# A 64-byte touch of B's first 256 rows ahead of the first loads of a fused matmul and RMSNorm

## The chip, the cores and the metric

The kernel runs on one core of one Trainium2 chip. The time is the device time of that core in microseconds (us), as a median over several executions. Beside the times there is a profile of one execution, whose span runs from the first to the last instruction that the profiler recorded.

## The reference

```python
def setup_inputs():
    m, k, n = 2048, 2048, 2048
    return {
        "a": np.random.randn(m, k).astype(np.float32),
        "b": np.random.randn(k, n).astype(np.float32),
        "gamma": np.random.randn(n).astype(np.float32),
        "eps": np.float32(1e-5),
    }

def reference(a, b, gamma, eps):
    x = np.matmul(a, b)
    rms = np.sqrt(np.mean(x ** 2, axis=-1, keepdims=True) + eps)
    return (gamma * x / rms).astype(np.float32)
```

A 2048 x 2048 product is followed by a normalisation of each of its rows and a multiplication with `gamma`.

## The kernel before

TensorE (PE) needs A with its columns on the partitions, so every block of A is transposed before it is used. B is loaded with its rows on the partitions and turned from float32 into bfloat16 by the load itself; such loads are issued by GpSimd (POOL). B stays in on-chip memory, in tiles `raw[j][kp]`: `j` is the left or right half of the columns, `kp` a pair of 128-row blocks, so a pair is 256 rows (`W2`), and there are `KP` = 8 pairs.

The work has two parts. In the **head**, the first four 128-row blocks of A (`HB` = 4) are multiplied with B while B is still coming in, pair by pair of rows: `stream` runs the matmuls of one `kp` for seven groups (row block, column chunk of 512) at once, with the weights in `head_at`, and `stream_in_parts` those of the eighth. Between them `transpose_head(kp + 1)` transposes the next piece of A (L168) and VectorE copies it into `head_at` (L173). In the first step it comes after twelve of the fourteen matmuls (L388). The **rest** goes through A's other twelve row blocks two at a time with seven products in place of eight (`group_half`, `product`, L285), while earlier rows are normalised and stored through SyncE's queue (SP).

The order of the work is written out by hand. At the very start:

- SyncE and ScalarE each issue one load, L93: the first 256 columns of the four row blocks of A, two blocks on each queue, as float32, into `a0f`.
- GpSimd issues `load_b(0, 0)` (L102), two loads of 128 rows of B and 1024 columns each; then, with `load_head(kp)` (L106 and L102), the piece of A for `kp` as bfloat16, into the region `early`, and two loads of B for the same rows, for `kp` = 1, 2 and 3. Later pieces follow one for each step of the head.
- PE runs eight matmuls on zeros (L147) to warm up, then `transpose_first` (L157) on `a0f`, whose results VectorE and ScalarE copy into `head_at` (L161), and then the head's matmuls.

`a0f` lies in the first third of `early`. The results of the head go to eight tiles `x_slot[0]` to `x_slot[7]`, each 128 x 1024 float32. `x_tile` hands them out in order; `x_slot[7]` belongs to row block 3 and the right half of the columns, and is first written in the stage that ends the head.

Of the kernel before, what the change touches and what calls it, by code (L numbers as in the profile page):

```python
# [17 lines left out]
def kernel(  # L18
# [13 lines left out]
    nc = tc.nc  # L32
    P = 128
# [4 lines left out]
    W2 = 2 * P  # L38
# [36 lines left out]
    x_slot = [consts.tile([P, HALF], FP32, name=f"x_{n}") for n in range(8)]  # L75
# [12 lines left out]
    def at(mb):  # L88
        return (at_even, at_odd)[(mb // 2) % 2][:, mb % 2]


    for h, queue in enumerate((nc.sync, nc.scalar)):
        queue.dma_start(out=a0f[:, 2 * h:2 * h + 2, :],  # L93
                        in_=a[2 * h * P:(2 * h + 2) * P, 0:W2].rearrange("(r p) k -> p r k", p=P))
# [761 lines left out]
```

## Time and profile before

| | us |
|---|---|
| median of 4 runs | 221.16 |
| lowest and highest | 220.88, 221.66 |
| the profiled execution, its time | 221.05 |
| its span | 219.3 |

| engine | busy us | share of the span |
|---|---|---|
| PE | 207.9 | 95% |
| VectorE (DVE) | 165.8 | 76% |
| ScalarE (ACT) | 126.9 | 58% |
| GpSimd (POOL) | 36.2 | 17% |

The profile's page gives busy times by engine, the DMA queues, the costliest groups of instructions, and the chain of work that ended last, followed back from the last instruction to what released each step. From the trace one can ask for that chain in order of time, for the instructions of a stretch in order of time (with the idle time before each and what ended it in square brackets), and for a table of stretches: for each the busy time of PE, PE's weight loads, DVE, ACT and POOL with the number of instructions, the granted clock of PE, the busy share of the 16 DMA engines and the GB/s that they moved. For loads that convert to bfloat16 the bytes are counted as they are written, half of what is read. A line of a DMA queue gives packets, MB and the time of its packets as a share of the 16 engines. Queue q0 is GpSimd's, q1 SyncE's, q10 ScalarE's.

### The profile page before, as it was taken

Reading aid. Unit: us, or ns where it says so; the run is one execution under the profiler, and the core shown is the slowest. Engines: PE = TensorE matmul, PEld = TensorE weight load, DVE = VectorE, ACT = ScalarE, POOL = GpSimd, SP = SyncE. Lnnn points to the kernel's source line nnn. Section 1 sums busy time; section 2 is a strip of 40 time slices with the busy share of each in tenths; the row PEclk is TensorE's granted clock in tenths of the full one; section 3 lists DMA queues with packets and bytes.
Section 4 is the critical chain, followed back from the end, with each engine's and each line's share of the span. In section 5 each row is a group of like instructions: output and inputs, shape, how many; then the busy total and the mean of one; then the engine's idle time right before and its main releaser. Section 6 shows DMA issues by size and latency. Waiting matters only on the chain.

```text
span 219.3 us, 3023 instructions
## 1 busy us (share of the span) xinstructions
PE 207.9 (95%) x1012; PEld 97.4 (44%) x1032; DVE 165.8 (76%) x326; ACT 126.9 (58%) x263; POOL 36.2 (17%) x75
## 2 busy tenths in 40 slices
PE   7799999999999999999999999999999999999970
PEld 3344544444455444444444444444444444444440
DVE  2128799999889998989794639846794659787771
ACT  2110002920599898688745996289747996334471
POOL 7544443433020002100200002000200000000040
PEclk9999999999999999999999999999999999999996
DMA  7999999999929697948799049955699249145045
GB/s 153 176 201 207 199 205 210 212 207 228 411 80 350 218 278 211 374 163 238 212 294 404 15 87 274 358 231 96 167 291 400 57 89 365 70 177 209 1 179 205
DMA packets 36864, 46.60 MB, mean 213 GB/s; under 512 B 22256, under 2 KB 26352, under 8 KB 35568
## 3 DMA queue, kind: packets, MB, share of 16 engines
q0 software_dynamic: 10608, 23.86, 43.9%
q1 hardware_dynamic: 25824, 22.02, 33.2%
q10 hardware_dynamic: 416, 0.52, 0.7%
q8 instruction: 8, 0.13, 0.2%
q14 instruction: 8, 0.07, 0.1%
HBM read 34.60 MB, written 16.78 MB: 234 GB/s over the span
## 4 chain that ended last, share of the span: by engine, by line
PE 91%; DMA 3%; issue 1%; ACT 1%; POOL 1%; DVE 0%; ACTq 0%; POOLq 0%
PE acc L285 71%; PE acc L388 16%; DMA early<-in_a_dram 3%; PE tbank L419 2%; PE tbank L168 2%; PE acc L800 1%; POOL b L102 0%; PE tbank L185 0%; PE acc L185 0%; ACT x L739 0%; DVE head_at L173 0%; ACT sq L803 0%; ACT rms L352 0%; POOL t_left masks.py:199 0%; POOL t_left masks.py:197 0%
## 5 line engine op out<-in xcount | busy, mean ns | idle before, releaser
L285 PE MATMUL acc<-b,s 128*128 128x512 bf16 x397 | 92.7, 379 | 0.7
L285 PEld LDWEIGHTS <-s 128*128 128x128 f16 (+1 forms) x512 | 49.9, 98 | 59.9 <-DVE s L260 0.4
L388 PE MATMUL acc<-b,head_at 128*128 128x512 bf16 x171 | 42.1, 379 | 1.5 <-DMA b<-in_b_dram 1.4
L303 ACT ACTIVATE sq<-x 128x512 bf16<-128x512 f32 x53 | 33.4, 630 | 6.9 <-DVE x L732 3.0
L370 DVE SCALAR_TENSOR_TENSOR x<-x,r,gamma_sb 128x1024 f32<-128x1024 f32 x28 | 34.9, 1281 | 0.7
L219 ACT ACTIVATE sq<-a 128x1024 bf16<-128x1024 f32 x24 | 25.3, 1053 | 2.3 <-DMA a<-in_a_dram 1.6
L388 PEld LDWEIGHTS <-head_at 128*128 128x128 bf16 x176 | 16.9, 98 | 20.6 <-issue 1.5
L242 ACT ACTIVATE head_at<-a,s 128x2048 f16<-128x2048 f32 x10 | 20.0, 1998 | 3.4 <-DVE s L229 3.3
L102 POOL DMA_DIRECT2D b<-in_b_dram x32 | 17.2, 540 | 20.6 <-DMA b<-in_b_dram 14.3
L430 ACT COPY x<-acc 128x512 f32<-128x512 f32 x5 | 2.9, 581 | 24.7 <-PE acc L388 24.7
L285 PEld LDWEIGHTS <-head_at 128*128 128x128 f16 (+1 forms) x112 | 11.0, 98 | 13.2
L285 PE MATMUL acc<-early,head_at 128*128 128x512 bf16 x63 | 14.4, 379 | 0.1
L285 PEld LDWEIGHTS <-at_even 128*128 128x128 f16 x96 | 9.4, 98 | 11.3
L285 PE MATMUL acc<-early,s 128*128 128x512 bf16 x56 | 14.2, 379 | 0.0
L260 DVE TENSOR_TENSOR s<-head_at 128x1024 f16<-128x1024 f16 (+5 forms) x22 | 13.4, 634 | 0.1
L616 DVE TENSOR_TENSOR x<-x,x 128x512 f32<-128x512 f32 x9 | 6.2, 693 | 8.8 <-ACT x L614 8.3
L127 POOL COPY pace<-x 128x1 f32<-128x1 f32 x4 | 1.6, 412 | 66.4 <-DVE x L625 65.0
L598 ACT COPY x<-acc 128x512 f32<-128x512 f32 x9 | 5.2, 573 | 11.5 <-PE acc L285 7.7
L173 DVE COPY head_at<-tbank 128x1024 bf16<-128x1024 bf16 x7 | 4.8, 691 | 9.0 <-PE tbank L168 9.0
L285 PE MATMUL acc<-t_left,s 128*128 128x512 bf16 x47 | 11.3, 379 | 0.1
L784 POOL TENSOR_SCALAR x<-x,r 128x512 f32<-128x512 f32 x1 | 2.7, 2655 | 51.2 <-DVE r L346 51.2
L276 DVE TENSOR_TENSOR b<-b 128x1024 bf16<-128x1024 bf16 x16 | 10.8, 685 | 0.2
(113 smaller groups left out, 236.9 us busy)
## 6 DMA issues: line engine op xcount, KB each, us to landing
out_dram<-x SPq DMA_DIRECT2D x29, 512.0 KB, 3.7
a<-in_a_dram POOLq DMA_DIRECT2D x10, 1024.0 KB, 8.8
b<-in_b_dram POOLq DMA_DIRECT2D x32, 256.0 KB, 9.9
a<-in_a_dram POOLq DMA_DIRECT2D x4, 512.0 KB, 9.8
early<-in_a_dram POOLq DMA_DIRECT2D x7, 256.0 KB, 10.0
gamma_sb<-in_gamma_dram POOLq DMA_DIRECT2D x2, 512.0 KB, 8.3
out_dram<-x SPq DMA_DIRECT2D x3, 256.0 KB, 2.6
out_dram<-a SPq DMA_DIRECT2D x1, 512.0 KB, 3.3
```

The lines of the kernel that those rows point to most:

```text
L102: nc.gpsimd.dma_start(out=raw[j][kp][:, t, :], in_=b[lo:lo + P, j * HALF:(j + 1) * HALF])
L173: nc.vector.tensor_copy(out=head_at[:, 2 * kp:2 * kp + 2, :, :], in_=view)
L219: nc.scalar.activation(out=junk, in_=a32[mb][:, h * HALF:(h + 1) * HALF], func=ACTF.Square, scale=2.0 ** -8, accum_out=n2[:, h:h + 1])
L242: nc.scalar.activation(out=a16[mb], in_=a32.pop(mb), func=ACTF.Copy, scale=factor.pop(mb))
L260: nc.vector.tensor_tensor(out=sum_of(g, s)[:, lo:hi, :], in0=x[:, lo:hi, :], in1=y[:, lo:hi, :], op=op)
L276: nc.vector.tensor_tensor(out=flat[:, 1:3, :], in0=flat[:, 1:3, :], in1=flat[:, 0::3, :], op=ALU.add)
L285: nc.tensor.matmul(bank, lhsT[:, kp, :], rhs, start=(start and kp == 0), stop=(kp == KP - 1), skip_group_check=not start)
L303: nc.scalar.activation(out=sq[:, 0:CH], in_=src, func=ACTF.Square, scale=inv_sqrt_n, accum_out=msq[mb][:, c:c + 1])
L370: nc.vector.scalar_tensor_tensor(out=x, in0=x, scalar=inverse_of[mb], in1=gamma_sb[:, h * HALF:(h + 1) * HALF], op0=ALU.mult, op1=ALU.mult)
L388: nc.tensor.matmul(bank, head_at[:, kt, r, :], head_rhs(c, kt), start=(kt == 0), stop=(kt == KT - 1))
L598: nc.scalar.copy(out=c, in_=one[1])
L616: nc.vector.tensor_tensor(out=t, in0=t, in1=x12, op=ALU.add)
```

## The change

One load is issued on SyncE's queue ahead of everything else of the kernel. It reads the first 16 float32 values, 64 bytes, of each of the rows 0 to 255 of B, and puts them into the first 32 columns of `x_slot[7]`, two rows of B on each partition. Nothing reads them there. The rest of the kernel is as before; A's first tiles follow on the same queue.

```diff
@@ -88,6 +88,9 @@
     def at(mb):
         return (at_even, at_odd)[(mb // 2) % 2][:, mb % 2]
 
+
+    nc.sync.dma_start(out=x_slot[7][:, 0:32].rearrange("p (t n) -> p t n", t=2),
+                      in_=b[0:W2, 0:16].rearrange("(t p) n -> p t n", p=P))
 
     for h, queue in enumerate((nc.sync, nc.scalar)):
         queue.dma_start(out=a0f[:, 2 * h:2 * h + 2, :],
```

## The prediction

> **What bounds the kernel now.** I read the page first, for the engine that is full and for the chain that ended last.
>
> ```profile
> PE 207.9 (95%) x1012; PEld 97.4 (44%) x1032; DVE 165.8 (76%) x326; ACT 126.9 (58%) x263; POOL 36.2 (17%) x75
> ...
> PE 91%; DMA 3%; issue 1%; ACT 1%; POOL 1%; DVE 0%; ACTq 0%; POOLq 0%
> ```
>
> PE is busy 95% of the span and makes up 91% of the chain; the DMA share of the chain, 3%, is one piece. The chain in order of time shows where that piece lies:
>
> ```profile
> 3.01 6.86 DMA early<-in_a_dram
> 9.86 0.05 issue
> 9.91 0.63 PE tbank L168 x8
> ```
>
> From 9.91 us on the chain is PE nearly without a break to 212.25 us, and the table by stages gives PE 17.89 of 18.00 us between 22 and 40 and 171.11 of 172 us between 40 and 212. So a load at the very start can change the time in one way: it moves the moment at which PE can begin `transpose_head(1)` (L168), now 9.91 us, and perhaps the small stalls in the two steps after it. The timeline of the start shows what PE does before:
>
> ```profile
> 1.44 3.23 PE L147 MATMUL acc<-sq 128*128 128x512 bf16 x8 [1.44 <-DVE pace L137]
> ...
> 4.50 0.60 PE L157 MATMUL tbank<-t_left,early 128*128 128x128 f32 x4
> ...
> 6.12 1.67 PE L388 MATMUL acc<-b,head_at 128*128 128x512 bf16 x7 [0.58 <-DMA b<-in_b_dram]
> ...
> 8.57 1.24 PE L388 MATMUL acc<-b,head_at 128*128 128x512 bf16 x5 [0.78 <-DMA b<-in_b_dram]
> ...
> 9.91 0.62 PE L168 MATMUL tbank<-identity,early 128*128 128x128 bf16 x8
> ```
>
> PE stands still three times: 0.58 us for the first 128 rows of B, 0.78 us for the next 128, and 0.59 us (the weight load's wait on `early` in the list of waits shows 0.6) for the second piece of A. That is 1.95 us, all of it waiting for GpSimd's loads, none for A's first tiles: those landed 3.1 and 3.4 us after their issue at 0.72 us, at 3.8 and 4.1 us, while PE was in its eight warming matmuls until 4.67 us.
>
> Then I asked how the DMA engines do in that time, by the microsecond (last two columns: busy share of the 16 engines, over 1 where packets overlap, and GB/s moved):
>
> ```profile
> 3.00:4.00 1.00, 1.00 (x4) 0.33 (x3) 0.36 (x2) 0.00 (x0) 1.00 (x3) 1.00 1.18 304
> 4.00:5.00 1.00, 1.00 (x8) 0.76 (x7) 0.00 (x0) 0.00 (x0) 1.00 (x3) 1.00 1.28 162
> 5.00:6.00 1.00, 0.54 (x5) 0.40 (x4) 0.76 (x2) 0.42 (x2) 1.00 (x2) 1.00 1.02 96
> 6.00:7.00 1.00, 0.88 (x5) 0.40 (x5) 0.00 (x0) 0.23 (x1) 1.00 (x3) 1.00 0.88 110
> ...
> 9.00:10.00 1.00, 0.90 (x6) 0.28 (x5) 0.00 (x0) 0.00 (x0) 0.34 (x1) 1.00 1.11 201
> ```
>
> This is the finding that the forecast hangs on. From 4 to 7 us GpSimd's queue has the engines to itself and they are as occupied as later, but they move 162, 96 and 110 GB/s where 201 is usual from 9 us on. The DMA queue's line for 5 to 6 us, and then the one for 10 to 10.5 us, put it in time for a packet:
>
> ```profile
> q0 software_dynamic: 56, 0.10, 102.1%
> ```
>
> ```profile
> q0 software_dynamic: 53, 0.11, 112.7%
> ```
>
> The first is 56 packets, 9 of them tiny: 1.021 x 16 us / 47 = 348 ns for a packet of 2 KB. The second, with one tiny packet: 1.127 x 8 us / 52 = 173 ns. What travels from 4 to 7 us is exactly B's rows 0 to 255, the rows that the change touches. B's later rows come in at the usual rate.
>
> [...] between 3 and 4 us the trace has all three queues at work, so the touch competes with everything. [...] so that the touch can help is supported by the trace's slow patch alone.
>
> **The change part by part.**
> *SyncE's issue.* One more DMA ahead of L93. The neighbour has the same number of runs (128 partitions x 2), and took 0.45 us to issue, so A's first half is issued at 1.17 instead of 0.72 us. Nothing else is queued on SyncE until the store at 70.76 us.
> *The touch's packets.* 256 of 64 bytes, 16 for each engine. No row of before shows 64-byte packets; the nearest are the 256-byte ones of SyncE's transposes between 76 and 76.5 us, and for the rate at which the queue starts, A's own between 1.8 and 2.3 us:
>
> ```profile
> q1 hardware_dynamic: 420, 0.11, 107.0%
> ```
>
> ```profile
> q1 hardware_dynamic: 91, 0.09, 62.6%
> ```
>
> The first is 1.07 x 8 / 420 = 20 ns each: 256 x 20 / 16 = 0.33 us of every engine. The second is 182 packets a us with the engines only 63% busy: should that be a limit of the queue, the touch holds A's half back by 256 / 182 = 1.4 us. So A's first half lands 0.45 + 0.33 = 0.8 us later (4.6 us), at worst 0.45 + 1.4 = 1.85 us later (5.65 us).
> *What that costs at A.* From the weight load at 4.29 us the transposes and copies take until 5.62 us, and PE then waits for B until 6.12. So a landing up to 4.3 us costs nothing, up to 4.8 us still nothing at the first matmul, and the two later waits (0.78 + 0.59 us) absorb 1.37 us more. A's half would have to be late by 0.5 + 0.5 + 1.37 = 2.3 us before 9.91 moves, if B comes as before. I take zero. If B comes earlier this cover goes: then A's lateness limits the gain.
> *What it costs at B.* The touch adds 0.33 us of engine time and pushes part of A's 256 packets past 3.4 us, where B's first packets start. At best it uses the idle time before 1.8 us and the 37% idle just after it, for 0.1 us; at worst all of A's half (256 x 46 ns / 16 = 0.74 us) runs beside B. I take 0.3 us later for everything on GpSimd's queue.
> *What it may bring.* From 4 to 7 us 0.368 MB moved; at 201 GB/s that takes 1.83 us, so the patch costs 1.17 us on average, and more on the slowest engine, which sets the landing. The upper end is set by PE: its first matmul can't come before 5.62 us and the twelve ahead of the transposes take 1.67 + 1.24 us, so 9.91 can't fall below 8.53, a gain of 1.4 us; the two landings after that (PE steps begin at 13.90 and 18.04, then 22.17, where the later ones are 3.98 us apart) could return another 0.3 us. The lower end is nothing. I take 1.35 us.
> *The tile.* `x_slot[7]` is next written by a ScalarE copy of the pair stage after 50 us; its wait on the touch is met long before. Zero.
> *Sum.* -1.35 + 0.3 = -1.05 us. The profiled execution took 221.05 us, span 219.3 and 1.75 around it, which is 0.11 below the median of 221.16; the change acts within the span, so the forecast is 221.16 - 1.05 = 220.1 us.
>
> **The rivals.**
> *The touch does not do it (slow patch of another origin).* GpSimd issues one load after another from 1.22 to 7.41 us, and the patch ends with that; A's first tiles, also a first read, ran at 311 and 304 GB/s. If the patch belongs to GpSimd's burst, only the costs stay: +0.1 to +0.85 us, about 221.4 us. Against it: later issues of the same kind, at 10.15 and 11.45 us, come with no slow packets.
> *Paid twice (slower).* The touch's reads are slow in themselves, as B's are now, and hold the engines, while B's bulk is none the faster. Place: all 16 engines before 4 us; price: up to the 1.17 us of the patch again, plus 0.3: about 222.6 us. It decides from the point where the touch costs each engine more than 0.66 us, that is 41 ns a packet, or where A's half lands over 2.3 + 0.66 us late.
> *The gain lands behind A.* The touch warms B but A's half comes at 5.65 us: PE's first transposes start 1.35 us late, the first matmul at about 7.0, the twelfth ends at 9.9, and hardly 0.1 us is left: 221.1 us.
>
> **How the numbers follow.** A measurement of this kernel can tell about 0.3% (0.66 us) from no change. The patch shortened: 0.52, own range 219.5 to 220.8 us; of that 0.46 is a gain over 0.66 us and 0.06 less, the case behind A included. No effect: 0.30, of that 0.24 within 0.66 us and 0.06 slower by more. Paid twice: 0.18, of that 0.17 slower by more and 0.01 within. Sums: faster 0.46, same 0.31, slower 0.23. The range 219.5 to 222.0 us leaves out about 0.05 below and 0.13 of the paid-twice case above.
>
> **What would show it.** Right: between 4 and 7 us about 200 GB/s, packets near 173 ns, L168's first run at 8.6 to 9.2 us, PE's waits for B shrunk from 1.36 us to under 0.6. The dead touch: the same 96 to 110 GB/s, L168 at 9.9 to 10.5 us. Paid twice: low GB/s also from 2 to 4 us and A's transposes (L157) starting after 5 us. A start of L168 that moves while the time doesn't would overturn the whole argument, since PE has no other slack in which to lose it.

## The result, and the profile after

| | before | after |
|---|---|---|
| median, us | 221.12 (48 runs) | 223.20 (29 runs) |
| lowest to highest, us | 220.65 to 223.16 | 221.44 to 227.96 |
| runs of 223.2 us or more | 0 of 48 | 15 of 29 |
| ratio of times, with 95% interval | | 1.0073 (1.0058 to 1.0088) |
| the profiled execution: time, span | 221.05, 219.3 | 221.44, 219.6 |

The ratio leaves out executions more than 1.5% above the fastest of their kernel, six of the 29 of after, and the same holds for the ratios below; medians, extremes and counts are over all. The change is slower, where 220.1 us was forecast, and its times are spread over 6.5 us. The profiled execution is the shortest of the 29, so it is read first, for a run in which little goes wrong.

The page of after, busy time by engine and the chain by engine:

```profile
PE 208.6 (95%) x1012; PEld 98.1 (45%) x1032; DVE 165.9 (76%) x326; ACT 126.9 (58%) x263; POOL 36.4 (17%) x75
...
PE 92%; DMA 3%; issue 1%; ACT 1%; DVE 0%; ACTq 0%; POOLq 0%
```

Nothing shows at this distance. Three lines were added to the code, so L168 of before is L171 here, L388 is L391, L157 is L160. The chain in order of time:

```profile
1.22 6.47 DMA b<-in_b_dram
7.69 0.04 issue
7.74 2.75 PE acc L391 x12
10.49 0.57 PE tbank L171 x8
```

The piece of DMA in the chain is now the load of B's first 128 rows, not the second piece of A. The timeline of the start:

```profile
0.72 0.48 ACTq L96 DMA_DIRECT2D early<-in_a_dram  x1
0.73 0.46 SPq L92 DMA_DIRECT2D x<-in_b_dram  x1
...
1.24 0.45 SPq L96 DMA_DIRECT2D early<-in_a_dram  x1
...
4.83 1.06 PE L160 MATMUL tbank<-t_left,early 128*128 128x128 f32 x4
...
7.74 2.75 PE L391 MATMUL acc<-b,head_at 128*128 128x512 bf16 x12 [1.26 <-DMA b<-in_b_dram]
...
10.43 0.62 PE L171 MATMUL tbank<-identity,early 128*128 128x128 bf16 x8
```

A's half on SyncE is issued at 1.24 us, 0.52 later. In this run that costs nothing: the later of A's two halves has landed at 4.13 us, where it had at 4.11 us before, and PE does not wait for A. PE's transposes begin 0.33 us later for another reason. The trace's record of the full clock begins at 6.07 us here and at 4.17 us before; ahead of it PE starts a warming matmul every 0.42 us, behind it a matmul of that size every 0.21 us, so the eight warming matmuls take longer. (The tables print a clock of 1.00 also where the trace has no record of it.) e9 below, without a touch, begins its transposes at 4.83 us too. The first matmul comes at 7.74 where it was 6.12 us: B's first rows land 1.6 us later than before. PE gets most of that back, since the second block of B is there when its turn comes and the twelve matmuls run in one go; `transpose_head(1)` starts at 10.43, 0.52 us late. The table by microsecond:

```profile
4.00:5.00 1.00, 1.00 (x4) 0.52 (x3) 0.00 (x0) 0.00 (x0) 1.00 (x3) 1.00 0.56 98
5.00:6.00 1.00, 1.00 (x7) 1.00 (x6) 0.07 (x1) 0.00 (x0) 1.00 (x2) 1.00 1.24 156
6.00:7.00 1.00, 0.48 (x4) 0.33 (x3) 0.68 (x2) 0.49 (x2) 0.67 (x2) 1.00 0.99 119
7.00:8.00 1.00, 0.26 (x2) 0.14 (x2) 0.00 (x0) 0.16 (x1) 0.02 (x1) 1.00 0.93 121
...
9.00:10.00 1.00, 1.00 (x6) 0.49 (x5) 0.00 (x0) 0.00 (x0) 0.53 (x1) 1.00 1.31 204
```

The slow patch is not shortened: it has moved from 4 to 7 us to 4 to 8 us, and at its beginning the 16 DMA engines are busy for only 0.56 of the time although loads of B are waiting. From 12 us on the two profiles do the same work in the same time: PE busy 28.79 and 28.84 us of 29 between 12 and 41 us, 167.16 us of 168 in both between 41 and 209 us.

### The profile page after: what moved, and what is told of

Same layout as the page of the kernel before. It is cut to its first block, busy times and chain, and to the rows that moved or that the text cites. A ratio compares the mean times of both kernels' runs of the same rounds, so it can differ in the third digit from the quotient of the medians.

```text
span 219.6 us, 3026 instructions
## 1 busy us (share of the span) xinstructions
PE 208.6 (95%) x1012; PEld 98.1 (45%) x1032; DVE 165.9 (76%) x326; ACT 126.9 (58%) x263; POOL 36.4 (17%) x75
## 4 chain that ended last, share of the span: by engine, by line
PE 92%; DMA 3%; issue 1%; ACT 1%; DVE 0%; ACTq 0%; POOLq 0%
PE acc L288 71%; PE acc L391 17%; DMA b<-in_b_dram 3%; PE tbank L422 2%; PE tbank L171 2%; PE acc L803 1%; PE tbank L188 0%; PE acc L188 0%; ACT x L742 0%; DVE head_at L176 0%; ACT sq L806 0%; ACT rms L355 0%; DVE r L349 0%; ACT a L742 0%; ACTq L806 0%
## 5 line engine op out<-in xcount | busy, mean ns | idle before, releaser
L391 PE MATMUL acc<-b,head_at 128*128 128x512 bf16 x171 | 42.0, 379 | 1.4 <-DMA b<-in_b_dram 1.3
L391 PEld LDWEIGHTS <-head_at 128*128 128x128 bf16 x176 | 16.9, 98 | 20.4 <-issue 1.4
```

Source lines behind the costliest of these rows:

```text
L391: nc.tensor.matmul(bank, head_at[:, kt, r, :], head_rhs(c, kt), start=(kt == 0), stop=(kt == KT - 1))
```

## The experiments

Each kernel was timed beside the kernel before on the same chip. A **long** run is one of 223.2 us or more, the median of after. Of the kernel before, 7 of 285 runs were long over all comparisons.

| kernel | runs | median, us | lowest to highest | long | ratio to before (95%) |
|---|---|---|---|---|---|
| e1 the change again | 22 | 222.38 | 221.78 to 225.78 | 8 | 1.0053 (1.0029 to 1.0078) |
| e2 touch of A's rows | 22 | 222.75 | 221.68 to 227.13 | 9 | 1.0046 (1.0022 to 1.0071) |
| e3 touch behind A | 14 | 221.62 | 221.04 to 223.00 | 0 | 1.0006 (0.9983 to 1.0028) |
| e4 one packet | 14 | 221.77 | 221.14 to 222.73 | 0 | 1.0006 (0.9984 to 1.0028) |
| e15 16 packets | 22 | 221.84 | 221.16 to 224.74 | 2 | 1.0021 (1.0007 to 1.0034) |
| e14 128 packets | 22 | 221.83 | 221.25 to 225.53 | 4 | 1.0024 (1.0006 to 1.0043) |
| e5 512 packets | 20 | 222.19 | 221.38 to 224.13 | 3 | 1.0038 (1.0017 to 1.0058) |
| e6 identity first | 22 | 223.19 | 221.51 to 225.99 | 11 | 1.0060 (1.0036 to 1.0085) |
| e11 one more memset | 22 | 223.43 | 221.62 to 227.10 | 13 | 1.0054 (1.0030 to 1.0079) |
| e13 two more memsets | 13 | 223.28 | 221.87 to 225.51 | 7 | 1.0075 (1.0052 to 1.0098) |
| e16 16 warming matmuls | 16 | 222.54 | 221.82 to 228.49 | 4 | 1.0058 (1.0034 to 1.0081) |
| e10 change, halves exchanged | 22 | 221.82 | 221.16 to 223.88 | 4 | 1.0013 (0.9988 to 1.0037) |
| e9 before, halves exchanged | 22 | 221.32 | 220.91 to 222.39 | 0 | 0.9996 (0.9979 to 1.0013) |
| e7 before, burst apart | 20 | 221.38 | 220.84 to 224.19 | 1 | 0.9993 (0.9976 to 1.0010) |

The medians of before in these comparisons were 221.35 (e1 to e4), 221.33 (e5 to e7), 221.46 (e9 to e11) and 221.32 us (e13 to e16).

### What the long runs are: e1, e17, e18 (the change itself)

> The changed kernel itself once more, for a second profile and more times. Theory 'B is held up' (the touch lengthens or delays the slow arrival of B's first 256 rows): median about 223 us, spread over several us, and in the profile the matmuls of the first step (L391) begin after 7 us, later the slower the run is; from 12 us on nothing differs. Rival 'PE's clock' (a longer wait of PE leaves it at its low clock for longer): the slow executions have a low mean clock, about 0.98, and the matmuls after the first wait are spaced at over 400 ns.

> The changed kernel, one more profile. 'A's half is caught': if the execution takes over 223.2 us, then PE's first transposes (L160) wait for `early` until after 6 us, and in SyncE's queue all but one or two of the 16 engines are through with A by 4.2 us; or PE waits over 2 us for B. If it takes under 222.5 us, L160 starts by 5 us.

> As e17_look: the changed kernel, one more profile, with the same two cases.

e1 repeated the spread, 221.78 to 225.78 us, with a profile of a short run. e17 and e18 took 226.74 and 224.14 us and show two different things; how the other long runs divide between the two is not known. PE's timeline in e17:

```profile
10.35 1.08 PE L160 MATMUL tbank<-t_left,early 128*128 128x128 f32 x4 [5.31 <-DMA early<-in_a_dram]
11.23 1.06 PE L160 MATMUL acc<-t_left,early 128*128 128x128 f32 x4
12.08 3.82 PE L391 MATMUL acc<-b,head_at 128*128 128x512 bf16 x12
15.74 0.61 PE L171 MATMUL tbank<-identity,early 128*128 128x128 bf16 x8
```

PE waited 5.31 us for A's first tiles: SyncE's half, issued at 1.24, landed 9.0 us later, at 10.2 us. The queues' lines for 4.2 to 8 us of the same run say why:

```profile
q0 software_dynamic: 326, 0.50, 100.5%
q1 hardware_dynamic: 34, 0.03, 3.4%
```

Of A's 256 packets on q1 some thirty ran only in this stretch, each alone among packets of GpSimd's queue, and seven more after it. Thirteen of the 16 engines had finished A by 3.8 us, as all of them had in the shortest run; the last three were done at 4.6, 6.3 and 9.9 us. On these most A packets took 46 to 59 ns, and where B's packets went at their ordinary 173 ns the next one of A started 0.21 us later; in the slow patch, where a packet of B took up to 1.9 us, the last of the three engines once paused for 1.2 us between two packets of A. The load landed at 10.2 us, 0.3 us behind the last of the three and 6.4 us behind the other thirteen, so here one engine in sixteen was enough. In the shortest run the trace has sixteen reports of the end of SyncE's half, from 3.84 to 4.13 us, and the half has landed with the last. The long profile of e2 (225.2 us, one engine until 7.3 us) and those of e6 and e11 show the same, with waits until 7.76, 7.09 and 7.01 us.

In e18 A is in time and B is late:

```profile
4.83 0.63 PE L160 MATMUL tbank<-t_left,early 128*128 128x128 f32 x4
...
9.08 4.03 PE L391 MATMUL acc<-b,head_at 128*128 128x512 bf16 x12 [3.18 <-DMA b<-in_b_dram]
12.95 0.61 PE L171 MATMUL tbank<-identity,early 128*128 128x128 bf16 x8
```

B's first rows landed 7.8 us after their issue, at 9.04 us. The wait of 3.18 us had a price of its own, seen in the granted clock (the eighth column) of the table by microsecond:

```profile
8.00:9.00 1.00, 0.00 (x0) 0.00 (x0) 0.00 (x0) 0.00 (x0) 0.00 (x0) 0.65 1.32 192
9.00:10.00 1.00, 0.92 (x3) 0.37 (x3) 0.00 (x0) 0.00 (x0) 0.68 (x1) 0.50 1.29 209
```

PE came out of the wait at half its clock, and the twelve matmuls took 4.03 us where the short run has 2.75: 1.28 us more. In e17 they took 3.82 us; its record of the full clock begins only at 14.23 us. All that is lost lies ahead of L171, and nothing gives it back:

| profiled execution | time | first transpose of A | first matmul | L168 / L171 | span |
|---|---|---|---|---|---|
| before | 221.05 | 4.50 | 6.12 | 9.91 | 219.3 |
| after | 221.44 | 4.83 | 7.74 | 10.43 | 219.6 |
| e18, the change | 224.14 | 4.83 | 9.08 | 12.95 | 222.4 |
| e17, the change | 226.74 | 10.35 | 12.08 | 15.74 | 225.0 |

L171 is later than L168 of before by 3.04 us in e18 and 5.83 in e17; the spans are longer by 3.1 and 5.7 us.

### Whose packets are slow: e2, e8, e12, e7

e2, other rows touched:

```diff
-                      in_=b[0:W2, 0:16].rearrange("(t p) n -> p t n", p=P))
+                      in_=a[HB * P:HB * P + W2, 0:16].rearrange("(t p) n -> p t n", p=P))
```

> The touch reads 64 bytes of each of A's rows 512 to 767 in place of B's rows 0 to 255; number, size, queue and place stay. If it matters that B's own rows are read twice within 2 us: back to 221.1 to 221.5 us. If any 256 small packets ahead of A do it: about 223 us, as wide a spread as the change.

Measured: as slow and as wide as the change. Which rows are touched doesn't matter.

e8, without a touch, a piece of A ahead on GpSimd's queue:

```diff
+    nc.gpsimd.dma_start(
+        out=ah(1), in_=a[0:HB * P, W2:2 * W2].rearrange("(r p) k -> p r k", p=P))
     load_b(0, 0)
...
-    load_head(1)
+    load_b(0, 1)
```

> The kernel before, without a touch, with the piece of A for the second step issued on GpSimd's queue ahead of B's first rows. It shows whose packets stall. If the slow patch belongs to B's first rows as such, A's 512-byte packets run at 60 ns each and the patch comes behind them. If it belongs to what GpSimd's queue moves first, whatever that is, A's packets from 3.5 to 5 us take well over 60 ns and B's behind them 173 ns. The time is 221 to 223 us, since B's rows land later.

Measured: 226.39 us. From 4 to 5 us A's packets ran at a median of 60 ns, as they do later; B's first 256 packets, now from 4.8 to 10 us, stalled:

```profile
7.00:8.00 1.00, 0.00 (x0) 0.00 (x0) 0.00 (x0) 0.00 (x0) 0.20 (x1) 1.00 1.12 94
8.00:9.00 1.00, 0.00 (x0) 0.00 (x0) 0.00 (x0) 0.00 (x0) 0.56 (x1) 0.72 0.89 107
```

So the patch isn't tied to the microseconds from 4 to 7, nor to whatever GpSimd's queue moves first. The expected time was missed by 3.4 us: PE waited 4.42 us for B and then had half its clock (0.50 from 9 to 12 us), 5.14 us for the twelve matmuls.

e12, without a touch, B's rows in another order:

```diff
-    load_b(0, 0)
+    load_b(0, 1)
...
-    load_head(1)
+    load_b(0, 0)
+    nc.gpsimd.dma_start(
+        out=ah(1), in_=a[0:HB * P, W2:2 * W2].rearrange("(r p) k -> p r k", p=P))
```

> The kernel before, without a touch, with GpSimd loading B's rows 256 to 511 first, then rows 0 to 255, then the piece of A. If the slow packets belong to B's rows 0 to 255: the first 256 packets take 173 ns, the next 256 stall. If they belong to the first 256 of these packets, whichever rows they carry: the first stall and the next take 173 ns. The time is 223 to 226 us, since PE gets its rows later.

Its table by microsecond (time 225.34 us), where rows 256 to 511 come first and rows 0 to 255 move from about 8 us on:

```profile
5.00:6.00 1.00, 1.00 (x7) 1.00 (x6) 0.07 (x1) 0.00 (x0) 1.00 (x2) 1.00 0.95 92
6.00:7.00 1.00, 0.59 (x4) 0.43 (x3) 0.68 (x2) 0.38 (x2) 0.71 (x2) 1.00 0.86 98
...
8.00:9.00 1.00, 0.00 (x0) 0.00 (x0) 0.00 (x0) 0.00 (x0) 0.75 (x1) 1.00 1.13 211
```

Rows 256 to 511, loaded first, go at 92 to 98 GB/s, and rows 0 to 255 behind them at 211. The slow packets are among the **first 256 of B's packets, whichever rows they carry**. Before, place and order had coincided. e12 is one execution, but read packet by packet it is clear: the mean of the first 256 is 234 ns and that of the next 256, rows 0 to 255, is 173 ns; in the profile of before these are 251 and 173 ns. Most of the 256 are not slow. Their median is 173 ns, as later; in the profile of before 66 of them took over 250 ns, the longest 2.2 us, and these 66 make up 47% of the packet time of the 256.

e7, without a touch, GpSimd's later loads held back:

```diff
-    for kp in range(2, 4):
-        load_head(kp)
...
     transpose_first()
+    wait_for(head_at[:, 1, HB - 1, 0:1])
+    for kp in range(2, 4):
+        load_head(kp)
```

> The kernel before, without a touch, with GpSimd's loads for the third and fourth step issued only after A's first tiles are transposed and copied (about 6 us), in place of in one burst until 7.4 us. If the slow packets of B between 4 and 7 us come from GpSimd's burst of issues: 173 ns a packet there, L168 before 9.3 us, about 220.3 us. If they don't: the same 100 to 160 GB/s, and 221.1 to 221.5 us.

GpSimd issued nothing between 4.9 and 6.5 us, and the patch stayed:

```profile
5.00:6.00 1.00, 0.64 (x6) 0.49 (x5) 0.75 (x2) 0.33 (x2) 0.21 (x7) 1.00 1.18 115
6.00:7.00 1.00, 0.23 (x2) 0.11 (x2) 0.00 (x0) 0.32 (x2) 0.62 (x2) 1.00 0.88 108
```

The time is that of before. The burst is not the cause either; what is, remains open.

### How much has to stand ahead of A: e3, e4, e15, e14, e5

e3, the touch behind A's half on SyncE's queue:

```diff
-    nc.sync.dma_start(out=x_slot[7][:, 0:32]...
     for h, queue in enumerate((nc.sync, nc.scalar)):
         queue.dma_start(out=a0f[:, 2 * h:2 * h + 2, :],
...
+    nc.sync.dma_start(out=x_slot[7][:, 0:32]...
```

> The same touch of B's rows, but behind A's first half on SyncE's queue. If A's delay behind the touch is the cost: back to 221.1 to 221.3 us. If the touch disturbs B's bulk load: 223 us or more, since its packets now run even closer to B's first ones (about 2.5 to 3.5 us).

Measured: no long run in 14, ratio 1.0006. All 256 packets are still there, and they do run beside B's first ones, until 4.2 us; PE's first matmul:

```profile
6.59 3.05 PE L392 MATMUL acc<-b,head_at 128*128 128x512 bf16 x12
```

So the long runs don't come from the packets or the second DMA as such, but from their place ahead of A.

The number of packets ahead of A was then varied. e4, one; e15, 16; e14, 128; e5, 512:

```diff
+    nc.sync.dma_start(out=x_slot[7][0:1, 0:16], in_=b[0:1, 0:16])        # e4
+    nc.sync.dma_start(out=x_slot[7][0:16, 0:16], in_=b[0:16, 0:16])      # e15
+    nc.sync.dma_start(out=x_slot[7][:, 0:16], in_=b[0:P, 0:16])          # e14
+    nc.sync.dma_start(out=x_slot[7][:, 0:64].rearrange("p (t n) -> p t n", t=4),
+                      in_=b[0:2 * W2, 0:16].rearrange("(t p) n -> p t n", p=P))  # e5
```

> A touch of one row, 64 bytes on one partition, in the same place of the queue. It keeps SyncE's 0.5 us of issue ahead of A's first half and the shift of every later load and store by one on its queue, without the 256 packets. If the issue or the shift is the cost: about 223 us. If the packets are: 221.1 to 221.4 us.

> A touch of 16 rows on 16 partitions: 16 packets, one for each DMA engine at most. SyncE's issue and the place in the queue are those of the change. 'A's half is caught' by the engine time ahead of it: as with one packet, 221.5 to 221.9 us, at most 1 in 20 over 223.2 us.

> A touch of 128 rows, one to each partition: 128 packets, 8 for each DMA engine, in place of 16. If the tail grows with the packets ahead of A: about half as many executions over 223.2 us as with 256 rows (there 23 of 51), median 222.0 us. If it is a matter of a second DMA being there: as with one packet, none over 223.2 us.

> The touch made twice as long: 64 bytes of each of B's rows 0 to 511, 512 packets. Theory 'A's half is caught' (A's first half now starts late enough that its last packets share the DMA engines with B's stalling first packets, and A has landed only when the slowest of 16 engines is through): A's half starts about 0.6 to 1.2 us later still, nearly every execution is caught, median 225 us or more. Rival 'B alone' (the touch only makes B's first 256 rows land later, A doesn't matter): about 0.3 us of engine time more, 223.0 us at most.

Long runs: 0 of 14, 2 of 22, 4 of 22, with 256 packets 23 of 51 (after and e1), with 512 only 3 of 20. With one to 128 packets the median is 0.4 to 0.5 us above that of before; with the touch behind A (e3) it is 0.3 us above, and the intervals of e3 and e4 include no change, so a price of any DMA ahead of A is not shown. Both lie 0.3 to 0.4 us above the ranges expected, and e15's two long runs are slightly more than the one in 20 expected. The share of long runs grows with the number up to 256, though neighbouring counts are too small to be told apart. The expectation for 512 failed on the wrong side: fewer long runs, not more, while e6, timed beside it, had 11 of 22. In its profile B's first packet starts at 3.86 us, later than the 3.5 to 3.75 of the change, and A is through by 4.1 us. That the later start of B spared A is a guess from one profile.

Nor is it enough that A's packets run beside B's first ones. In the profile of before, 37 packets of A, all of ScalarE's half, start after B's first packet and are through at 3.75 us; in that of e4 it is 77 packets of SyncE's half, through at 3.80 us, about as many as the 76 of e17. What makes a few of them wait on one engine in some runs and not in others is not known.

### Exchanging A's halves: e9, e10

```diff
-    for h, queue in enumerate((nc.sync, nc.scalar)):
+    for h, queue in enumerate((nc.scalar, nc.sync)):
```

> The kernel before, without a touch, with the two queues' halves of A's first tiles exchanged: ScalarE's queue loads rows 0 to 255, SyncE's rows 256 to 511. In all kernels so far whose first half of A started late (about 2.7 us in place of 1.8) B's first packets stalled and B's first tile landed 1.2 us later. Theory 'the later queue': SyncE's queue still starts first, nothing changes, 221.1 to 221.5 us. Rival 'which rows' (A's rows 0 to 255 read just ahead of B's rows 0 to 255 slow these): rows 0 to 255 now start last, B's first packets stall, L168 at 10.4 us or later, 221.8 us or more.

> The change with the same exchange: behind the touch on SyncE's queue now stand A's rows 256 to 511. 'The later queue': as the change, 222.3 to 223.2 us with a wide spread. 'Which rows': B's first packets run as before, and about 221.5 us.

e9 is equal to before, so which half SyncE loads doesn't matter without a touch. Yet in its profile (221.52 us) B's first tile came as late as in after:

```profile
4.83 1.06 PE L157 MATMUL tbank<-t_left,early 128*128 128x128 f32 x4
...
7.91 2.75 PE L388 MATMUL acc<-b,head_at 128*128 128x512 bf16 x12 [1.16 <-DMA b<-in_b_dram]
10.49 0.61 PE L168 MATMUL tbank<-identity,early 128*128 128x128 bf16 x8
```

So B can be this late without anything ahead of A, and the 0.52 us by which L171 is late in the profile of after can't be put down to the touch. e10 lies between before and the change, with 4 long runs of 22; its interval overlaps that of e1, so it decides nothing.

### Taking B's packets away from A: e6, e11, e13

```diff
# e6: make_identity ahead of load_b(0, 0)
# e11:
+    nc.gpsimd.memset(x_slot[6][:, 0:CH], 0.0)
     load_b(0, 0)
# e13:
+    nc.gpsimd.memset(x_slot[6], 0.0)
+    nc.gpsimd.memset(x_slot[5][:, 0:CH], 0.0)
     load_b(0, 0)
```

> The touch stays; GpSimd builds the identity (0.6 us) before it issues its first load of B in place of after, so B's first packets start about 0.6 us later, when A's half is through. 'A's half is caught': the long runs go, the highest stays under 223.5 us although B is issued later, the median is 222 to 222.6 us. 'B alone': everything is later by the 0.6 us, median about 223.3 us, with the same spread.

> The change with one more GpSimd instruction (zeros into 512 columns of x_slot[6], which nothing reads) ahead of its first load of B, so that this is issued 0.6 to 0.9 us later than in the change and its packets start after A's half is through on all 16 engines (about 4 us). 'A's half is caught between B's packets': the executions over 224 us go and the spread shrinks to that of the kernel before, at a median of 222 to 222.8 us. If A's tail comes from anything else: spread stays, median 223.5 us or more.

> The change with more GpSimd work ahead of its first load of B (zeros into x_slot[6] and half of x_slot[5], which nothing reads; about 1.6 us, of which 0.5 fall into time before the first issue), since in the two earlier tries that load was not issued later than 1.42 us. Now B is issued at about 2.3 us and its first packets come at about 4.5 us, behind all of A's. 'A's half is caught': PE's first transposes (L160) start by 5 us in every execution, so the long runs go: none over 224 us, highest minus lowest under 2 us, at a median of 222.5 to 223.3 us for B's lateness. If the long runs stay: A's lateness has another cause.

None did what it was meant to do. In e6 and e11 the added work fell into time in which GpSimd hadn't issued anyway: B was issued at 1.42 and 1.25 us against 1.22. In e13 it was issued at 2.08 us, and still its first packet started at 3.68 us, no later than in the change. So e6 and e11 are in effect the change once more, long runs included, and the direct test, A without B's packets beside it, wasn't had. e13's profile (223.91 us) is of the kind of e18: a wait of 2.01 us for B, then a granted clock of 0.50 from 8.89 us on and 4.44 us for the twelve matmuls.

### PE's clock: e16

```diff
-    for _ in range(8):
+    for _ in range(16):
         nc.tensor.matmul(warm_bank, ...
```

> The change with sixteen warming matmuls in place of eight (their result is used nowhere), so that PE is busy until about 6.5 us and its clock is up when A's half comes late. If the low clock after the long wait makes half of the loss in the long runs (12 matmuls took 4.77 us in the long run of the touch on A's rows, 2.75 in the short ones): highest under 225.5 us, median 222.3 to 222.8 us. If the clock has no part: highest 226 to 228 us as in the change, and a median that is higher by up to 0.4 us, since the transposes start later.

Inconclusive: the median fits the first case, but one run took 228.49 us, with 4 long ones of 16. The clock's part is known from traces alone: in the long profiles of e17, e18, e2, e6 and e11 the twelve matmuls took 3.52 to 4.77 us in place of 2.75.

## Why the prediction was wrong, point by point

**The gain (forecast 1.35 us, measured none).** The step that failed is the reading of the slow patch: "exactly B's rows 0 to 255, the rows that the change touches". In after these rows still came at 98 to 156 GB/s. They were also the first of B's packets, and e12 shows that order decides, not place. The forecast asked which rows the slow packets carried, and not in what order they came. It also read its 348 ns, the mean of one microsecond, as the time of a packet; packet by packet most take 173 ns and a quarter stall. The rival that the touch does nothing was right about the slow patch, wrong in the cause that it named, GpSimd's burst (e7), and its 221.4 us was too low. The prediction's own doubt, that only the slow patch spoke for the touch, was in place; the runs do show a cost at the start of B's loads, a mean of 251 ns for the first 256 packets against 173 for the next in before, but not one that the touch takes away: 257 ns in after.

**The touch's own packets (20 ns taken).** Smaller. SyncE's queue in after, 1.8 to 2.3 us:

```profile
q1 hardware_dynamic: 251, 0.02, 30.9%
```

0.309 x 8 us / 251 = 9.8 ns a packet, so 256 x 9.8 / 16 = 0.16 us of each engine in place of 0.33. The rival "Paid twice" has the nearest time, 222.6 us, but its mechanism, slow 64-byte reads, is refuted by this line, so that nearness is luck. The last of its conditions was met in some runs, though: A's half more than 2.96 us late, by 6.4 us in e17, from waiting and not from slow reads.

**A's half (cost taken as zero).** The term most mis-sized. The issue was nearly right (0.52 us later for 0.45 forecast), and in the shortest run zero was right too. The bound "at worst 1.85 us late" was a bound on an average engine, against a cover of 2.3 us. In e17 A landed at 10.2 us where before had 3.8, 6.4 us late. e17 shows the two things that were left out of account for A: its packets, 46 to 59 ns each, started 0.21 us apart between B's of 173 ns, and three engines were done at 4.6, 6.3 and 9.9 us where the other thirteen were by 3.8. The prediction let the slowest engine set the landing of B's rows, and didn't do so for A.

**B's first rows (0.3 us taken).** In the shortest run they land 1.6 us later, of which 0.52 us reaches L171, as in e9 without a touch; in e18 3.0 us later (first matmul 9.08 against 6.12). e4's ratio of 1.0006 and e15's of 1.0021 put the ordinary share, with no or few long runs, at 0.1 to 0.5 us, so 0.3 us was a fair size for it.

**PE's clock (no term).** It was left out. In e18, where PE stood still from 5.90 to 9.08 us, the granted clock is full from 4.88 to 8.30 us and half from 8.30 to 11.71, 3.41 us each, and the twelve matmuls took 1.28 us more than the 2.75 of the shortest run. In e13 half the clock followed a wait of 2.01 us, as the last section says.

**The argument about where it counts.** Right: span and L168/L171 move together (e18 and e17), and behind that point nothing gives the loss back or adds to it. The tile cost nothing, as forecast: between 41 and 209 us PE is busy for 167.16 us in both profiles.

**What stays open:** why some of B's first 256 packets stall; why they come more slowly still in the profile of after (0.56 of the engines busy from 4 to 5 us; 0.95 in e9); how often a long run is A's wait and how often B's; and, as it couldn't be taken away, whether B beside A is the cause of A's long waits. The traces show it in each of the four profiles of that kind (e17, e2, e6, e11), but no experiment removed it alone, and A runs beside B without harm in before and e4.

## What to carry to other kernels

A small DMA placed ahead of a load that the first instructions wait for may be paid not by its bytes but by where it pushes that load. Here 256 packets that took 0.16 us of each engine made 23 of 51 runs long, against none of 14 with the same packets behind that load. In the long profiles the last packets of A on one to three engines of 16 waited among those of a slow neighbour, or B itself was late, and PE stood still for two to five microseconds. Bound the lateness of a load by its slowest engine and by the longest packet seen beside it, not by the mean, and look at the spread of the times as well as at one profile. Before a slow stretch is put down to which data it moves, change the order of the transfers once: order and place look the same in a single trace.

## What the runs showed of the hardware that was not expected

- Of B's first 256 packets (4 KB read, 2 KB written), 21 to 38% take over 250 ns in each of the 20 profiles, the longest of a profile between 0.6 and 3.2 us, and their mean is 234 to 294 ns; the next 256 have a mean of 172 to 178 ns. It is so whichever rows they carry (e12) and also when they start at 4.8 us (e8).
- B's first packet starts between 3.3 and 3.9 us in all profiles in which B's loads come first on GpSimd's queue, although their issue was moved from 1.22 to 2.08 us (e13).
- PE's clock fell behind a stretch in which PE was partly at work: in e13 it was full from 5.48 to 8.89 us, where PE worked 0.7 us at the start and 0.7 us at the end, and half (0.50) for the next 3.41 us. In after, with 2.15 us of work in the 3.41 us from the start of its record of the full clock (6.07 to 9.48 us), it stayed at 1.00.
